# Input projection of an encoder block: a pair's results are made behind the next pair's fourth product, and one of two query or key tiles is convolved in the second half

## The chip, the cores and the metric

The kernel runs on one core of a Trainium2 chip. Five engines with queues of their own work side by side: PE (TensorE, the matrix multiplies), DVE (VectorE), ACT (ScalarE), POOL (GpSimd) and SP (SyncE, which issues all transfers here). The metric is the time of one execution on the device in microseconds (us), lower is better; several executions are run and their median is given.

## The reference, cut to what matters

One layer of a bidirectional encoder block on x of 2048 tokens and 1024 channels. All columns come out of one input projection, and queries and keys go through a short convolution along the tokens:

```python
h = rms_norm(x, norm_pre_g)
proj = einsum('bsd,de->bse', h, w_in)
u_a, z_a, q, k, v, o, z_b, gates, g_a, g_b = split(proj, split_points)
...
qk = silu(centred_depthwise_conv(concatenate([q, k]), conv_qk_w, conv_qk_b))   # 5 taps
q, k = split(qk)
...
h_fwd = mlstm_direction(qh, kh, vh, i_pre[0], f_pre[0])
h_bwd = flip(mlstm_direction(flip(qh), flip(kh), flip(vh), ...))
...
out = einsum('bsd,de->bse', sigmoid(g_a + b_merge[0]) * p_a + sigmoid(g_b + b_merge[1]) * p_b, w_out)
return x + rms_norm(out, norm_post_g)
```

Everything is float32. The change touches only what lies before the recurrences (`mlstm_direction`).

## The kernel before

`phase1` (L434) is the input projection. The tokens are taken in two halves of `HALF` = 1024, each half in two blocks of `BLK` = 512. The columns of the weight are taken in 36 pairs of 128 columns (`in_pairs`, L48). Each pair has a kind: q, k, v and u (a query, key, value or pooling-branch pair) have much to do behind the products, z, o, ga and gb (gates) little; these latter are called light here. The pairs are in a fixed order: ga0 gb0 q0 v0 k0 o0 z0 q1 o1 k1 v1 o2 u0 z1 u1 o3 v2 q2 o4 z2 k2 o5 u2 v3 o6 u3 z3 q3 o7 gb2 k3 ga3 gb3 ga1 gb1 ga2. The first two are computed plainly, the other 34 by a form of Strassen's product (`strassen`, L369): seven products instead of eight, of sums and differences of quarters of the weights (made by DVE at L352, split into a high and a low part by ACT and POOL, L93 and L97) and of x.

A product is 12 matmuls of 128x128 by 128x512 (`mm3`, lines 105 to 107: high by high, high by low, low by high, for four k tiles). The products write to three PSUM banks A, B and C, each with two buffers. Below, P1 to P7 are the seven in the order of the code, of which P2, P4 and P6 use bank B and the engines read the banks like this: ACT copies P1 to `p1`; DVE makes `u2` = bank B + p1 after P2 (L394), and `u3` = bank B + p1 after P4 has been added into the bank (L399). After P6 has been added too, out(2) reads bank B; out(3) reads P3's bank C with u3, out(1) P7's bank C with u2, and out(0) bank A. The out functions make the four tiles of 128 channels by 512 tokens.

`strassen` is a generator, and the main loop interleaves two pairs: `next(this)` issues P1 and P2 of pair i, `run(rest)` issues P6 and P7 of pair i-1 and all that is made of that pair, and the second `next(this)` issues P3, P4, P5 of pair i:

```python
this = work(i, W)
next(this)
run(rest)
next(this)
rest = this
```

So PE sees P1 P2 of a pair, then P6 P7 of the pair before, then P3 P4 P5. P6 of a pair cannot start before u3 of that pair has been read out of bank B.

What is made of a pair: `pair_qk` (L586) has two raw tiles of 128 channels by 1024 tokens (with a halo), and convolves each: ACT makes the first tap with the bias (L602), DVE the other four (L606, scalar_tensor_tensor), ACT a sigmoid (L610), POOL the multiply (L611), SP stores the result. `pair_v` (L613) transposes its raw tiles on PE (L625, 16 transposes of 128x128 into PSUM tiles `vtr`), and ACT and DVE write high and low parts (`vnh`, `vnl`), whose extra columns DVE clears (L618, L619). `pair_u` (L632) makes window sums. The light pairs make a sigmoid and a multiplication or two (L707, L719, L721). Tiles come from pools with three buffers each for raw and acc (all results, among them acc, vnh, vnl, zs, gB) and six for p1, u2, u3.

In the second half the weights are not prepared but reloaded (`again_w`, L308; `keep_w`, L338, stores them in the first). At pairs 10 and later of that half `masked` (L857) makes 32 decay tiles `nm` for a later stage.

The order on each engine is not written by hand: a scheduler places the instructions by the order of the code, by priorities (`tc.high_priority`), by its own timeline of costs and by free buffers; `tc.issue_after(ins)` keeps an instruction behind another. 

Of the kernel before, what the change touches and what calls it, by code (L numbers as in the profile page):

```python
# [77 lines left out]
class Kernel:  # L78
    def __init__(self, ctx, tc, a):
        self.ctx, self.tc, self.nc, self.a = ctx, tc, tc.nc, a  # L80
        self.n = 0
        self.plain = None
        self.free = {}
# [224 lines left out]
    def again_w(self, W, i, wr, wc):  # L308
# [23 lines left out]
        read = nc.sync.dma_start(b22, w_in[i, :, 4:8, P:])  # L332
        put("B22", b22, "pool")
        return read
# [34 lines left out]
    def strassen(self, H, W, psum, pool, out, n=BLK, swap=False):  # L369


        nc = self.nc
# [21 lines left out]
        nc.vector.tensor_tensor(u2, bank["B"], p1, op=ALU.add)  # L394
# [4 lines left out]
        nc.vector.tensor_tensor(u3, bank["B"], p1, op=ALU.add)  # L399
        out(3, bank["C"], u3)  # L400
# [5 lines left out]
        out(2, bank["B"], p1)  # L406
        prod("C", "S4", "B22", False)
        out(1, bank["C"], u2)

# [24 lines left out]
    def phase1(self):  # L434
        tc, nc, a = self.tc, self.nc, self.a
        with ExitStack() as es:
# [6 lines left out]
            wt = es.enter_context(tc.tile_pool(name="wt", bufs=3))  # L443
            po = {t: es.enter_context(tc.tile_pool(name=f"po_{t}", bufs=3)) for t in ("raw", "acc", "p")}
            self.rows = es.enter_context(tc.tile_pool(name="rows", bufs=1))
            self.decay = es.enter_context(tc.tile_pool(name="decay", bufs=2))
# [10 lines left out]
            n = len(self.pairs)  # L457
            for half in range(2):
# [50 lines left out]
                for i in range(2, n):  # L509
# [8 lines left out]
                    with tc.high_priority(offset=200):  # L518
# [3 lines left out]
                        else:  # L522
                            read = self.again_w(W, i, wr, wc)
                    if half == 1:
                        with tc.issue_after(read.ins):
                            for u in range(max(0, 8 * (i - 10) // 6), max(0, min(32, 8 * (i - 9) // 6))):
                                self.masked(u, mask)
# [3 lines left out]
                    this = work(i, W)  # L531
# [3 lines left out]
                    rest = this  # L535
                run(rest)
# [34 lines left out]
    def collect(self, H, W, psum, pool, width, off):  # L571
# [4 lines left out]
        def out(i, ps, add):  # L576
            d = t[i % 2][:, off + (i // 2) * BLK : off + (i // 2 + 1) * BLK]
            if add is None:
                nc.scalar.activation(d, ps, AF.Copy)
            else:  # L580
                nc.vector.tensor_tensor(d, ps, add, op=ALU.add)
# [4 lines left out]
    def pair_qk(self, half, kind, h, H, W, psum, pool):  # L586
        nc = self.nc
        t = yield from self.collect(H, W, psum, pool, HALF + 6, 2 if half == 0 else 4)
        n = HALF - 2 if half == 0 else HALF + 2
        tstart = 0 if half == 0 else HALF - 2  # L590
        dst = self.sp[f"{kind}T{h}"]
        for i in range(2):
            raw = t[i]
            ct = (8 if kind == "k" else 0) + 2 * h + i
            if half == 0:
                nc.vector.memset(raw[:, 0:2], 0.0)  # L596
                nc.vector.tensor_copy(self.halo_qk[:, ct, :], raw[:, HALF - 2 : HALF + 2])
            else:
                nc.vector.tensor_copy(raw[:, 0:4], self.halo_qk[:, ct, :])
                nc.vector.memset(raw[:, HALF + 4 : HALF + 6], 0.0)  # L600
            acc = pool.tile([P, HALF + 2], F32, tag="acc", name=self.nm("acc"))
            nc.scalar.activation(  # L602
                acc[:, :n], raw[:, 0:n], AF.Identity, scale=self.cw[:, ct, 0:1], bias=self.cb[:, ct : ct + 1]
            )
            for tap in range(1, TAPS):
# [4 lines left out]
            nc.scalar.activation(raw[:, :n], acc[:, :n], AF.Sigmoid)  # L610
            nc.gpsimd.tensor_tensor(acc[:, :n], acc[:, :n], raw[:, :n], op=ALU.mult)  # L611
            nc.sync.dma_start(dst[:, i, tstart : tstart + n], acc[:, :n])
# [55 lines left out]
    def pointwise(self, H, W, psum, pool, body):  # L668
# [3 lines left out]
        def out(i, ps, add):  # L672
            if add is None:
                body(i % 2, i // 2, ps)
            else:
                nc.vector.tensor_tensor(add, ps, add, op=ALU.add)
                body(i % 2, i // 2, add)

        yield from self.strassen(H, W, psum, pool, out)

    def pair_z(self, half, kind, g, H, W, psum, pool):
        nc = self.nc
        o = [pool.tile([P, HALF], F32, tag="acc", name=self.nm("zs")) for _ in range(2)]

        def body(i, b, x):
            d = o[i][:, b * BLK : (b + 1) * BLK]
# [7 lines left out]
    def pair_g(self, half, kind, g, H, W, psum, pool):  # L694
# [4 lines left out]
        def out(i, ps, add):  # L699
# [3 lines left out]
            else:  # L703
                x = d = add
                nc.vector.tensor_tensor(x, ps, add, op=ALU.add)
# [3 lines left out]
            nc.sync.dma_start(dst[:, i % 2, t0 : t0 + BLK], d)  # L709

        yield from self.strassen(H, W, psum, pool, out)

    def pair_o(self, half, kind, j, H, W, psum, pool):
        nc = self.nc
        o = [pool.tile([P, HALF], F32, tag="acc", name=self.nm("gB")) for _ in range(2)]

        def body(i, b, x):
            d = o[i][:, b * BLK : (b + 1) * BLK]
# [8 lines left out]
    def spills(self):  # L727
# [11 lines left out]
        for i in range(2, len(self.pairs)):  # L739
            sp[f"wt{i}"] = self.dram(f"wt{i}", [P, 4, 2, 4 * P])  # L740
        for j in range(8):
# [793 lines left out]
```

## Time and profile before

| | us |
|---|---|
| median of 3 executions | 2410.05 (2406.89 to 2412.60) |
| the profiled execution, its own time | 2414.79 |
| its span in the trace | 2413.0 |
| PE busy | 2325.3 (96%) |
| DVE busy | 1477.7 (61%) |
| POOL busy | 1139.3 (47%) |
| ACT busy | 895.5 (37%) |

Busy time is the time in which an engine executes an instruction; the span is from the first to the last record of the trace. In a timeline, a row gives the start, the duration, the instruction with its output and inputs, and in square brackets how long the engine was idle before it and which instruction's end released it. A matmul's duration overlaps that of the next, so the step from start to start is the measure there. The input projection fills about the first 1430 us, half of it each of the two halves of the tokens.

### The profile page before, as it was taken

To read this page: it belongs to the slowest core of one execution; us is meant where nothing else is said; L and a number is where in the kernel's file an instruction comes from. 1 tells how busy PE (TensorE), PEld (TensorE's weight loads), DVE (VectorE), ACT (ScalarE), POOL (GpSimd) and SP (SyncE) were. 2 spreads that over 40 slices of the span, in tenths; PEclk is the share of its full clock that TensorE was granted. 3 is DMA by queue.
4 is the path that set the end of the run, shared out by engine and by line. 5 is a ranking of instruction groups with operands and counts; after the bars stand their busy time and mean duration, and the time that the engine had idled before them with its cause. 6 is when DMAs were issued, how large, how long until landed. Compare 5 with 4: busy or idle time off the path is not lost. (4 is left out here: it accounts for less than half of the span.)

```text
span 2413.0 us, 35767 instructions
## 1 busy us (share of the span) xinstructions
PE 2325.3 (96%) x12569; PEld 2003.2 (83%) x12569; DVE 1477.7 (61%) x2495; ACT 895.5 (37%) x1773; POOL 1139.3 (47%) x902
## 2 busy tenths in 40 slices
PE   7998999999999999999999999998999999999998
PEld 5777788887878778888888887997989899999776
DVE  6886766887875465534465433887985333354765
ACT  5434333433334333222322333776764112121442
POOL 4655655564655423544454430554564211233775
PEclk9999999999999999999999999999999999999999
DMA  4457565556684466787777766766656546588763
GB/s 155 167 207 240 205 237 214 219 173 220 219 278 171 141 191 201 235 264 233 246 227 241 253 226 232 228 209 216 205 184 212 173 154 200 182 282 278 250 218 122
DMA packets 300707, 513.24 MB, mean 213 GB/s; under 512 B 27248, under 2 KB 137968, under 8 KB 300528
## 3 DMA queue, kind: packets, MB, share of 16 engines
q1 hardware_dynamic: 300528, 510.97, 63.4%
q8 instruction: 99, 1.62, 0.3%
q14 instruction: 80, 0.66, 0.1%
HBM read 314.25 MB, written 196.61 MB: 212 GB/s over the span
## 5 line engine op out<-in xcount | busy, mean ns | idle before, releaser
L606 DVE SCALAR_TENSOR_TENSOR acc<-raw,conv_w,acc 128x1022 f32<-128x1022 f32 (+1 forms) x128 | 219.0, 1735 | 10.4 <-ACT acc L602 6.9
L97 POOL TENSOR_TENSOR wB21l<-wraw,wB21h 128x512 fp32r<-128x512 f32 x76 | 109.8, 1445 | 228.4 <-ACT wB21h L93 200.5
L1159 POOL TENSOR_TENSOR qs<-q,isc 128x256 f32<-128x256 f32 x120 | 92.2, 771 | 143.3 <-PE num L1175 62.6
L97 POOL TENSOR_TENSOR wB22l<-wraw,wB22h 128x512 fp32r<-128x512 f32 x76 | 118.0, 1552 | 81.6 <-ACT wB22h L93 61.9
L885 PE MATMUL pb<-oxs,w_proj_mlstml 128*128 128x256 f32 x512 | 143.8, 281 | 0.0
L884 PE MATMUL pb<-oxs,w_proj_mlstmh 128*128 128x256 f32 x512 | 143.8, 281 | 0.0
L884 PE MATMUL paps<-pys,w_proj_poolh 128*128 128x256 f32 x512 | 143.4, 282 | 0.2 <-POOL pys L97 0.2
L883 PE MATMUL pb<-oxs,w_proj_mlstmh 128*128 128x256 f32 x512 | 143.5, 280 | 0.0
L883 PE MATMUL paps<-pys,w_proj_poolh 128*128 128x256 f32 x512 | 142.3, 282 | 0.6 <-DVE sga L1012 0.6
L885 PE MATMUL paps<-pys,w_proj_pooll 128*128 128x256 f32 x512 | 142.1, 282 | 0.0
L394 DVE TENSOR_TENSOR u<-bankB,p 128x512 f32<-128x512 f32 x76 | 52.1, 686 | 138.6 <-PE bankB L107 128.9
L97 POOL TENSOR_TENSOR wB11l<-wraw,wB11h 128x512 fp32r<-128x512 f32 x72 | 109.8, 1526 | 40.5 <-ACT wB11h L93 39.1
L105 PE MATMUL bankB<-A22h,wT4h 128*128 128x512 f32 x272 | 108.5, 399 | 14.0 <-DVE u L399 14.0
L611 POOL TENSOR_TENSOR acc<-acc,raw 128x1022 f32<-128x1022 f32 (+1 forms) x32 | 79.6, 2487 | 71.1 <-ACT raw L610 63.7
L105 PE MATMUL bankC<-S1h,wT1h 128*128 128x512 f32 x272 | 107.6, 395 | 3.4 <-ACT sg L707 3.4
L105 PE MATMUL bankB<-S3h,wT3h 128*128 128x512 f32 x272 | 106.2, 390 | 2.7 <-DVE u L394 2.7
L107 PE MATMUL bankB<-A22h,wT4l 128*128 128x512 f32 x272 | 108.0, 397 | 0.0
L106 PE MATMUL bankB<-A22l,wT4h 128*128 128x512 f32 x272 | 108.0, 397 | 0.0
L107 PE MATMUL bankB<-S2h,wT2l 128*128 128x512 f32 x272 | 106.7, 392 | 1.2 <-DVE raw L596 1.2
L107 PE MATMUL bankC<-S1h,wT1l 128*128 128x512 f32 x272 | 107.2, 394 | 0.0
L105 PE MATMUL bankB<-S2h,wT2h 128*128 128x512 f32 x272 | 107.1, 394 | 0.0
L106 PE MATMUL bankC<-S1l,wT1h 128*128 128x512 f32 x272 | 106.9, 393 | 0.0
(438 smaller groups left out, 7662.5 us busy)
## 6 DMA issues: line engine op xcount, KB each, us to landing
wraw<-in_w_in SPq DMA_DIRECT2D x110, 512.0 KB, 4.3
wt<-wT2h SPq DMA_DIRECT2D x34, 256.0 KB, 3.5
wt<-wT1h SPq DMA_DIRECT2D x34, 256.0 KB, 3.7
wt<-wT3h SPq DMA_DIRECT2D x34, 256.0 KB, 3.8
wt<-wT2l SPq DMA_DIRECT2D x34, 256.0 KB, 3.6
wt<-wT1l SPq DMA_DIRECT2D x34, 256.0 KB, 3.6
wt<-wT3l SPq DMA_DIRECT2D x34, 256.0 KB, 2.6
wt<-wT4h SPq DMA_DIRECT2D x34, 256.0 KB, 2.0
```

The lines of the kernel that those rows point to most:

```text
L97: return eng.tensor_tensor(lo, x, hi.bitcast(F32), op=ALU.subtract)
L105: nc.tensor.matmul(ps, wh, xh, start=start and kt == 0, stop=False, skip_group_check=True)
L106: nc.tensor.matmul(ps, wh, xl, start=False, stop=False, skip_group_check=True)
L107: nc.tensor.matmul(ps, wl, xh, start=False, stop=stop and kt == 3, skip_group_check=True)
L394: nc.vector.tensor_tensor(u2, bank["B"], p1, op=ALU.add)
L606: nc.vector.scalar_tensor_tensor(acc[:, :n], raw[:, tap : tap + n], self.cw[:, ct, tap : tap + 1], acc[:, :n], op0=ALU.mult, op1=ALU.add,)
L611: nc.gpsimd.tensor_tensor(acc[:, :n], acc[:, :n], raw[:, :n], op=ALU.mult)
L883: nc.tensor.matmul(ps, wh, xh, start=i == 0, stop=False)
L884: nc.tensor.matmul(ps, wh, xl, start=False, stop=False)
L885: nc.tensor.matmul(ps, wl, xh, start=False, stop=i == n)
L1159: nc.gpsimd.tensor_tensor(qs[d], q[:, :, ck], isc[:, d, j % 2, None, :].to_broadcast([P, 2, P]), op=ALU.mult)
```

## The change

Two things are changed. First, `strassen` yields once more behind u3 and once at its end, and the loop has more steps: P1, P2 of pair i; P6, P7 of pair i-1; P3, P4 and u3 of pair i; then what is made of pair i-1; then out(3), P5 and out(0) of pair i. Second, in the first half only tile 0 of each q or k pair is convolved; the raw tile 1 is stored to DRAM. In the second half it is loaded again into a pool with one buffer of its own, `late` (`late_load`, behind pair i's last weight load, from pair 5 on), and convolved (`conv`) in a later light pair, each tap kept behind one of the four DVE instructions of that pair that read banks (`read_banks`). So 8 tiles are convolved at another time, with 8 stores and 8 loads of 512 KB more. Besides, zs and gB tiles are taken when first written, nm lives in the pool of the weight differences (three buffers) instead of decay's two, and decay has one buffer.

```diff
@@ strassen
-        nc.vector.tensor_tensor(u2, bank["B"], p1, op=ALU.add)
+        self.read_banks.append(nc.vector.tensor_tensor(u2, bank["B"], p1, op=ALU.add))
         yield
         prod("C", "S1", "T1", True)
         prod("B", "S3", "T3", False)
         u3 = pool.tile([P, n], F32, tag="p", name=self.nm("u3"))
-        nc.vector.tensor_tensor(u3, bank["B"], p1, op=ALU.add)
-        out(3, bank["C"], u3)
+        self.read_banks.append(nc.vector.tensor_tensor(u3, bank["B"], p1, op=ALU.add))
+        yield
+        self.read_banks.append(out(3, bank["C"], u3))
         if not self.edge:
             prod("A", "A12", "B21", False)
             out(0, bank["A"], None)
         yield
         prod("B", "A22", "T4", False)
-        out(2, bank["B"], p1)
+        self.read_banks.append(out(2, bank["B"], p1))
         prod("C", "S4", "B22", False)
         out(1, bank["C"], u2)
+        yield
...
@@ phase1
+            late, waits = [(kind, h) for h in range(NH) for kind in "qk"], None
...
-                    this = work(i, W)
+                    this, self.read_banks = work(i, W), []
+                    next(this)
+                    next(rest, None)
                     next(this)
                     run(rest)
                     next(this)
                     rest = this
+                    if half == 1 and waits is not None and i >= 7 and self.pairs[i][0] not in "qkuv":
+                        kind, h, raw = waits
+                        self.conv(pool, kind, h, 1, raw, HALF - 2, 0, self.read_banks)
+                        waits = None
+                    elif half == 1 and waits is None and late and i >= 5:
+                        with tc.issue_after(self.read.ins):
+                            waits = self.late_load(*late.pop(0))
...
@@ pair_qk
             if half == 0:
-                nc.vector.memset(raw[:, 0:2], 0.0)
                 nc.vector.tensor_copy(self.halo_qk[:, ct, :], raw[:, HALF - 2 : HALF + 2])
+                if i == 1:
+                    nc.sync.dma_start(self.sp[f"raw{kind}{h}"], raw[:, 2 : HALF + 2])
+                else:
+                    nc.vector.memset(raw[:, 0:2], 0.0)
+                    self.conv(pool, kind, h, i, raw, HALF - 2, 0)
...
+    def conv(self, pool, kind, h, i, raw, n, tstart, ties=()):
...
+        for tap in range(1, TAPS):
+            with self.tc.issue_after(ties[tap - 1].ins) if ties else ExitStack():
                 nc.vector.scalar_tensor_tensor(
                     acc[:, :n], raw[:, tap : tap + n], self.cw[:, ct, tap : tap + 1], acc[:, :n],
                     op0=ALU.mult, op1=ALU.add,
                 )
...
+    def late_load(self, kind, h):
+        raw = self.late.tile([P, HALF + 2], F32, tag="late", name=self.nm("late"))
+        self.nc.vector.memset(raw[:, 0:2], 0.0)
+        self.nc.sync.dma_start(raw[:, 2:], self.sp[f"raw{kind}{h}"])
+        return kind, h, raw
...
@@ masked
-        t = self.decay.tile([P, 2, 2, P], F32, tag="nm", name=self.nm("nm"))
+        t = self.wt_pool.tile([P, 2, 2, P], F32, tag="wt", name=self.nm("nm"))
```

What this does to the order of the engines is shown at three places. The first is DVE's queue in the first half where q1 (raw_1674 and raw_1675, with the accumulators acc_1918 and acc_1929) meets u3 of o1 (u_311_1962). Before, from q1's last raw on:

```order
L581 TENSOR_TENSOR raw_1675<-bankC_1678,u_270_1705 128x512
L606 SCALAR_TENSOR_TENSOR acc_1918<-raw_1674,conv_w,acc_1918 128x1022 x2
L606 SCALAR_TENSOR_TENSOR acc_1929<-raw_1675,conv_w,acc_1929 128x1022
L606 SCALAR_TENSOR_TENSOR acc_1918<-raw_1674,conv_w,acc_1918 128x1022
L352 TENSOR_TENSOR wt_2152<-wraw_2134,wraw_2132 128x512
L606 SCALAR_TENSOR_TENSOR acc_1929<-raw_1675,conv_w,acc_1929 128x1022
L399 TENSOR_TENSOR u_311_1962<-bankB_1860,p_307_1874 128x512
L606 SCALAR_TENSOR_TENSOR acc_1918<-raw_1674,conv_w,acc_1918 128x1022
L606 SCALAR_TENSOR_TENSOR acc_1929<-raw_1675,conv_w,acc_1929 128x1022
L676 TENSOR_TENSOR u_311_1962<-bankC_1861,u_311_1962 128x512
L606 SCALAR_TENSOR_TENSOR acc_1929<-raw_1675,conv_w,acc_1929 128x1022
```

And now, with the lines of the changed kernel (L595 is out of a q, k or v pair, L628 a tap, L400 u3, L705 and L756 belong to o1); tile 0's accumulator is acc_1935:

```order
L595 TENSOR_TENSOR raw_1668<-bankC_1671,u_268_1698 128x512
L628 SCALAR_TENSOR_TENSOR acc_1935<-raw_1667,conv_w,acc_1935 128x1022 x3
L352 TENSOR_TENSOR wt_2136<-wraw_2118,wraw_2116 128x512
L628 SCALAR_TENSOR_TENSOR acc_1935<-raw_1667,conv_w,acc_1935 128x1022
L400 TENSOR_TENSOR u_305_1931<-bankB_1851,p_303_1865 128x512
L705 TENSOR_TENSOR u_305_1931<-bankC_1852,u_305_1931 128x512
L756 TENSOR_TENSOR gB_1948<-u_305_1931,gB_1948 128x512
L98 TENSOR_TENSOR wT2l_2129<-wt_2126,wT2h_2128 128x512
L395 TENSOR_TENSOR u_335_2043<-bankB_2015,p_334_2029 128x512
```

Two accumulators were worked on side by side, five taps ahead of u3 and three behind it; now there is one, with all four taps ahead of u3.

The second place is PE's queue in the first half, where v0 (raw_992 and raw_993) is transposed while k0 is computed. Before, at the start of P3 of k0 (bankC_1165):

```order
L105 MATMUL bankC_1165<-S1h_393,wT1h_1129 128x512
L106 MATMUL bankC_1165<-S1l_394,wT1h_1129 128x512
L625 MATMUL vtr_1224<-ident,raw_992 128x128
L625 MATMUL vtr_1231<-ident,raw_992 128x128
L107 MATMUL bankC_1165<-S1h_393,wT1l_1130 128x512
L105 MATMUL bankC_1165<-S1h_393,wT1h_1129 128x512
```

and at the end of its P4 (bankB_1164):

```order
L105 MATMUL bankB_1164<-S3h_395,wT3h_1135 128x512
L106 MATMUL bankB_1164<-S3l_396,wT3h_1135 128x512
L625 MATMUL vtr_1224<-ident,raw_993 128x128
L625 MATMUL vtr_1224<-ident,raw_992 128x128
L625 MATMUL vtr_1224<-ident,raw_993 128x128
L625 MATMUL vtr_1231<-ident,raw_993 128x128
L625 MATMUL vtr_1231<-ident,raw_992 128x128
L625 MATMUL vtr_1231<-ident,raw_993 128x128
L107 MATMUL bankB_1164<-S3h_395,wT3l_1136 128x512
L105 MATMUL bankA_1163<-A12h_389,wB21h_1139 128x512
```

Now (raw_1003 and raw_1004, L654) at the end of P4:

```order
L108 MATMUL bankB_1166<-S3h_406,wT3l_1138 128x512
L654 MATMUL vtr_1252<-ident,raw_1003 128x128
L654 MATMUL vtr_1252<-ident,raw_1004 128x128
L654 MATMUL vtr_1252<-ident,raw_1003 128x128
L654 MATMUL vtr_1252<-ident,raw_1004 128x128
L654 MATMUL vtr_1259<-ident,raw_1003 128x128
L654 MATMUL vtr_1259<-ident,raw_1004 128x128
L654 MATMUL vtr_1259<-ident,raw_1003 128x128
L654 MATMUL vtr_1259<-ident,raw_1004 128x128
L106 MATMUL bankA_1165<-A12h_400,wB21h_1141 128x512
```

The first two transposes moved from the start of P3 to the end of P4, and the other six from ahead of P4's last matmul to behind it.

The third place is DVE's queue in the second half, in the changed kernel only, where the late convolution of light pair o1 (late_7389, acc_7908) meets the next pair, k1; L395 is u2 and L400 u3 of k1, and the L705 and L756 belong to o1:

```order
L395 TENSOR_TENSOR u_1391_7980<-bankB_7952,p_1390_7966 128x512
L705 TENSOR_TENSOR p_1361_7800<-bankB_7786,p_1361_7800 128x512
L705 TENSOR_TENSOR u_1362_7814<-bankC_7787,u_1362_7814 128x512
L628 SCALAR_TENSOR_TENSOR acc_7908<-late_7389,conv_w,acc_7908 128x1022
L756 TENSOR_TENSOR gB_7892<-u_1362_7814,gB_7892 128x512
L628 SCALAR_TENSOR_TENSOR acc_7908<-late_7389,conv_w,acc_7908 128x1022 x2
L400 TENSOR_TENSOR u_1392_8035<-bankB_7952,p_1390_7966 128x512
L628 SCALAR_TENSOR_TENSOR acc_7908<-late_7389,conv_w,acc_7908 128x1022
L595 TENSOR_TENSOR raw_7950<-bankC_7953,u_1392_8035 128x512
```

Three of the four late taps, which are new here, stand between u2 and u3 of k1, and the fourth behind u3.

## Rows read from the trace of the kernel before

**Rows 1.** The page: busy time and share of each engine.

```profile
PE 2325.3 (96%) x12569; PEld 2003.2 (83%) x12569; DVE 1477.7 (61%) x2495; ACT 895.5 (37%) x1773; POOL 1139.3 (47%) x902
```

**Rows 2.** Windows: PE, PEld, DVE, ACT, POOL busy, clock, DMA share, GB/s.

```profile
200.00:300.00 100.00, 87.99 (x367) 70.65 (x366) 76.15 (x84) 42.20 (x69) 58.98 (x36) 0.95 0.63 222
900.00:1000.00 100.00, 100.00 (x445) 82.85 (x444) 56.83 (x62) 33.43 (x50) 44.45 (x26) 1.00 0.68 218
```

**Rows 3.** Waits of PE, 60 to 760 us: total, times, longest.

```profile
PE bankB L105 <- DVE u L399: 13.2, 4, 4.7
...
PE vtr L625 <- DVE vnh L618: 3.2, 2, 1.6
...
PE vtr L625 <- DVE raw L581: 1.3, 1, 1.3
PE vtr L625 <- ACT raw L579: 1.2, 2, 0.8
```

**Rows 4.** Waits of PE, 760 to 1440 us.

```profile
PE vtr L625 <- DVE vnl L97: 2.6, 2, 2.5
PE vtr L625 <- DVE raw L581: 1.5, 1, 1.5
```

**Rows 5.** Timeline of PE: start, us, instruction, [idle before <-releaser].

```profile
212.96 0.79 PE L105 MATMUL bankB<-A22h,wT4h 128*128 128x512 f32 x1 [4.70 <-DVE u L399]
...
221.30 0.39 PE L105 MATMUL bankC<-S1h,wT1h 128*128 128x512 f32 x1
...
237.26 0.50 PE L105 MATMUL bankB<-A22h,wT4h 128*128 128x512 f32 x1 [2.20 <-DVE u L399]
...
239.21 0.39 PE L107 MATMUL bankB<-A22h,wT4l 128*128 128x512 f32 x1
...
278.90 0.50 PE L105 MATMUL bankB<-A22h,wT4h 128*128 128x512 f32 x1 [2.99 <-DVE u L399]
...
281.24 0.63 PE L107 MATMUL bankB<-A22h,wT4l 128*128 128x512 f32 x1
...
286.12 0.39 PE L105 MATMUL bankC<-S1h,wT1h 128*128 128x512 f32 x1
...
716.92 0.50 PE L105 MATMUL bankB<-A22h,wT4h 128*128 128x512 f32 x1 [3.31 <-DVE u L399]
```

**Rows 6.** Timeline of DVE, q1's taps.

```profile
225.74 7.97 DVE L606 SCALAR_TENSOR_TENSOR acc<-raw,conv_w,acc 128x1022 f32<-128x1022 f32 x4
```

**Rows 7.** Source line L606, 900 to 1400 us: ns min/median/max.

```profile
L606 DVE SCALAR_TENSOR_TENSOR acc<-raw,conv_w,acc x49: 1273/1289/3436, 899.9 to 1399.0; 128x1026 f32<-128x1026 f32 x49
```

**Rows 8.** Timeline of DVE, k1's taps.

```profile
269.63 5.74 DVE L606 SCALAR_TENSOR_TENSOR acc<-raw,conv_w,acc 128x1022 f32<-128x1022 f32 x3
```

**Rows 9.** Timeline of PE, transposes of v0 and v1.

```profile
140.88 0.88 PE L625 MATMUL vtr<-ident,raw 128*128 128x128 f32 x6 [1.54 <-DVE vnh L618]
...
294.08 0.88 PE L625 MATMUL vtr<-ident,raw 128*128 128x128 f32 x6 [1.64 <-DVE vnh L618]
```

**Rows 10.** Timeline of DVE, v0 of the first half.

```profile
133.60 0.07 DVE L619 MEMSET vnl<- 128x8 f32 x1 [0.52 <-DMA qT<-acc]
...
135.56 0.06 DVE L596 MEMSET raw<- 128x2 f32 x1 [1.26 <-POOL acc L611]
```

**Rows 11.** DVE groups, 800 to 1420 us: busy, mean ns, idle before.

```profile
L394 DVE TENSOR_TENSOR u<-bankB,p 128x512 f32<-128x512 f32 x31 | 21.3, 688 | 97.3 <-PE bankB L107 90.9 <-issue 6.4
L399 DVE TENSOR_TENSOR u<-bankB,p 128x512 f32<-128x512 f32 x30 | 20.6, 686 | 33.1 <-PE bankB L107 33.1
```

**Rows 12.** Timeline of POOL near 209 us.

```profile
209.27 1.27 POOL L97 TENSOR_TENSOR wT4l<-wt,wT4h 128x512 fp32r<-128x512 f32 x1 [3.58 <-ACT wT4h L93]
```

**Rows 13.** Timeline of DVE, a light pair of the second half.

```profile
967.84 3.44 DVE L606 SCALAR_TENSOR_TENSOR acc<-raw,conv_w,acc 128x1026 f32<-128x1026 f32 x1
...
980.56 0.69 DVE L399 TENSOR_TENSOR u<-bankB,p 128x512 f32<-128x512 f32 x1 [3.06 <-PE bankB L107]
...
988.79 0.69 DVE L394 TENSOR_TENSOR u<-bankB,p 128x512 f32<-128x512 f32 x1 [6.74 <-PE bankB L107]
```

More of the change, by code (lines that the diff above doesn't have):

```diff
@@ L82, in __init__ @@
         self.plain = None
+        self.read_banks = []
         self.free = {}
@@ L522, in phase1 @@
                         else:
-                            read = self.again_w(W, i, wr, wc)
+                            self.again_w(W, i, wr, wc)
                     if half == 1:
-                        with tc.issue_after(read.ins):
+                        with tc.issue_after(self.read.ins):
                             for u in range(max(0, 8 * (i - 10) // 6), max(0, min(32, 8 * (i - 9) // 6))):
@@ L600, in pair_qk @@
                 nc.vector.memset(raw[:, HALF + 4 : HALF + 6], 0.0)
[L601 to L605, printed above, removed]
+                self.conv(pool, kind, h, i, raw, HALF + 2, HALF - 2)
+    def conv(self, pool, kind, h, i, raw, n, tstart, ties=()):
+        nc = self.nc
+        ct = (8 if kind == "k" else 0) + 2 * h + i
+        acc = pool.tile([P, HALF + 2], F32, tag="acc", name=self.nm("acc"))
+        nc.scalar.activation(
+            acc[:, :n], raw[:, 0:n], AF.Identity, scale=self.cw[:, ct, 0:1], bias=self.cb[:, ct : ct + 1]
+        )
+        for tap in range(1, TAPS):
+            with self.tc.issue_after(ties[tap - 1].ins) if ties else ExitStack():
                 nc.vector.scalar_tensor_tensor(
@@ L682, in pair_z @@
         nc = self.nc
-        o = [pool.tile([P, HALF], F32, tag="acc", name=self.nm("zs")) for _ in range(2)]
+        o = []
         def body(i, b, x):
+            if not o:
+                o.extend(pool.tile([P, HALF], F32, tag="acc", name=self.nm("zs")) for _ in range(2))
             d = o[i][:, b * BLK : (b + 1) * BLK]
@@ L709, in out @@
             nc.sync.dma_start(dst[:, i % 2, t0 : t0 + BLK], d)
+            return None if add is None else read
         yield from self.strassen(H, W, psum, pool, out)
@@ L714, in pair_o @@
         nc = self.nc
-        o = [pool.tile([P, HALF], F32, tag="acc", name=self.nm("gB")) for _ in range(2)]
+        o = []
         def body(i, b, x):
+            if not o:
+                o.extend(pool.tile([P, HALF], F32, tag="acc", name=self.nm("gB")) for _ in range(2))
             d = o[i][:, b * BLK : (b + 1) * BLK]
@@ L740, in spills @@
             sp[f"wt{i}"] = self.dram(f"wt{i}", [P, 4, 2, 4 * P])
+        for h in range(NH):
+            for kind in "qk":
+                sp[f"raw{kind}{h}"] = self.dram(f"raw{kind}{h}", [P, HALF])
         for j in range(8):
```

28 lines of the change are left out of this document (13 added, 15 removed).

## The prediction

> **What bounds the kernel now.** I read the page first. PE is busy for 96% of the span [rows 1], so the time can move only where PE stands idle, where it runs at the lower clock, or where it gets another amount of work. The change gives PE the same instructions as before. Beyond the input projection (which fills the first 1430 us) no engine's order differs, so everything is decided there. The windows come next [rows 2]: in the second half PE is busy 100.00 of 100 us with 445 matmuls, so one matmul step is 100/445 = 0.225 us. In the first half, between 200 and 300 us, PE is busy only 87.99 us, its granted clock averages 0.95, and DVE is at 76.15 us. That window also holds the start of the q/k pairs.
>
> Then the waits of PE alone. In the first half [rows 3] the largest group is bankB waiting for the DVE instruction u3 of L399, 13.2 us in four waits. P6 of the pair before cannot write into bank B before u3 has read it, and u3 stands in DVE's queue behind convolution taps. The transposes of v (vtr) wait 3.2 us for vnh, 1.2 for ACT's raw and 1.3 for DVE's raw. In the second half there are just two groups, 2.6 and 1.5 us [rows 4]. These rows make 23 us in all, and only those waits that the change touches count.
>
> The four u3 waits one by one [rows 5]: 4.70 us before 212.96, 2.20 before 237.26, 2.99 before 278.90, 3.31 before 716.92. A long wait costs twice. After the 2.99 us the granted clock falls to the lower level: a matmul that takes 0.39 us at full clock takes 0.63 at 281.24, and the 24 matmuls of P6 and P7 from 278.90 to 286.12 take 7.22 us instead of 24 x 0.225 = 5.40, so 1.8 more. After the 2.20 us wait the matmuls stay at 0.39 (239.21). After the 4.70 us wait the 24 take 8.34, so 2.9 more.
>
> **The change part by part.**
>
> *One tile of two convolved in the first half.* The waits at 237.26 and 278.90 belong to o1 behind q1 and to v1 behind k1. The order shows for the first that five taps stand between q1's last raw and u3 of o1 before, and four afterwards, none of them behind u3. The weight difference (L352) stays between them. Four taps there took 7.97 us, so 1.99 each [rows 6]; a tap alone takes 1.29, the median of the second half [rows 7]. One tap fewer is worth 1.29 to 1.99; beside the same POOL work I take 1.7. **Term 1, q1/o1: -1.7** of 2.20, without clock. **Term 2, k1/v1:** three taps took 5.74, so 1.91 each [rows 8]; again -1.7 of 2.99. That leaves 1.3 us, less than the 2.20 after which no clock was lost, so the 1.8 us of clock come back too: -3.5. Bounds: -1.3 to -2.0 for term 1, and for term 2 -1.3 (a tap, and the clock falls all the same) to -4.8 (the whole wait).
>
> *What is made of a pair stands later.* This concerns v, whose 16 transposes are PE work. Before, in v0 of the first half, the first two of eight transposes stand behind the second matmul of P3 and wait 0.77 us for a raw of ACT (part of the 1.2 us group [rows 3]); afterwards all eight stand behind the last matmul of P4, 22 matmuls or 5 us later for these two, so that wait goes. The other six move by one matmul only, 0.2 us; what they wait 1.54 us for [rows 9] is DVE's last raw. Before, clears that wait for a store and for POOL's multiply stand ahead of it in DVE's queue [rows 10]; afterwards they don't, but two weight differences more do. I take half, 0.8. **Term 3, v0: -1.6** (0 to -2.3). **Term 4, v1:** 0.5 and 1.64 [rows 3, 9]; DVE's queue still holds clears of v's buffers, which wait for a store, ahead of raw. Half again, -0.9 (0 to -2.1). **Term 5, v3:** the 1.3 us on DVE's raw [rows 3]; DVE is behind with u2's window sums, which the change leaves, -0.2 (0 to -1.3). **Term 6, v0 of the second half:** 2.6 and 1.5 [rows 4]. u3 and the reading of bank C now stand ahead of the two vnl, 2 x 0.69 us later (20.6 us over 30 of them [rows 11]), against 3 more matmuls that PE has by then, 0.68. I take +0.7 (-2.5 to +2.5).
>
> *What stays.* The 4.70 us at 212.96: DVE waits there for a weight difference whose buffer POOL frees late, and POOL's instruction waited 3.58 us for ACT [rows 12]; none of these moves, 0. The 3.31 at 716.92 lies behind x of the second half (five L193), in the same order after: 0.
>
> *The second half gets eight convolutions.* 32 taps of 1.29 us are 41 us of DVE, put into a stretch in which DVE is busy 56.83 of 100 us [rows 2] and idles 97.3 us ahead of u2 and 33.1 ahead of u3 while PE works [rows 11]. That idle time is the cover. The dangerous place is the pair behind a light one, where three late taps stand ahead of u3, as the third order listing shows. Take k1 around 980 us, the pair of that listing [rows 13]: u3 starts at 980.56 as soon as P4 ends; PE needs the bank only after P5, P1 and P2, whose end shows as the start of the next u2, 988.79. Were all three taps to begin only at 980.56, u3 would end at 980.56 + 3 x 1.29 + 0.69 = 985.1, which leaves 3.7 us. Nothing is lost: 0. If the cover went, three taps would cost what lies above these 3.7 us.
>
> *DMAs.* Eight stores and eight loads of 512 KB, 8.4 MB against 513 MB, on SP's queue while the DMA engines are 0.63 to 0.68 busy [rows 2]; each load has a pair or more (some 19 us) before its taps: 0. The lazily taken zs and gB tiles and nm's buffers: 0 by the same cover; they gate nothing that PE waits for in these rows.
>
> **Sum:** -1.7 - 3.5 - 1.6 - 0.9 - 0.2 + 0.7 = -7.2 us. Against the profiled execution's own 2414.8 that gives 2407.6; this one lay 4.7 above the median 2410.05, so by the median's level the forecast is **2403 us**. With every bound taken favourably it is -2.0 - 4.8 - 2.3 - 2.1 - 1.3 - 2.5 = -15.0, unfavourably -1.3 - 1.3 + 2.5 = -0.1.
>
> **A rule against it.** In the trace one tap of the second half took 3.44 us against 1.29 [rows 13, 7], so something can hold a tap 2.15 us. The Trainium skill, page "SBUF — State Buffer", section "SBUF: two separate sides", says that VectorE with two SBUF inputs and a GpSimd instruction that reads SBUF lock each other out of a shared port pair for a whole instruction. The trace agrees in kind with this 3.44. By the rule every late tap could be held by a POOL instruction, and the change would cost time instead of nothing; by the medians it costs nothing.
>
> **Rivals.**
>
> *R1, no change that can be measured.* The waits merely pass over: u3 of o1 and v1 still has four taps at 1.9 and the weight difference ahead, the transposes wait for vnh wherever they stand. For it: DVE at 76% in that window [rows 2], and POOL-stretched taps. Against it: one tap less is certain in the order. The sum is then between -1.3 x 2 and -4.5: 2406 to 2411.
>
> *R2, slower.* The late taps are held beside POOL. Three of 3.44 are 10.3 us against 3.9, 6.5 more, above the 3.7 of slack by 2.8; with lost clock (1.8) 4.6 us a convolution. From 3.7 us of extra hold (two of three taps) it decides. In half of the eight it costs 18 us, 2421; in all, 37 us, 2440. Against it: the median of 49 taps is 1.289 [rows 7] and POOL is busy 44.45% there [rows 2].
>
> *R3, more gain.* With half of the convolution gone from the first half, ACT and POOL come earlier, and the 4.70 + 2.9 at 212.96 or the 3.31 at 716.92 with slow matmuls behind it (1.8, as behind 278.90) shrink: 5 to 10 us beyond the forecast, 2393 to 2398. Against it: the chains there [rows 12] aren't made of convolution work in the order.
>
> **How the numbers follow.** Forecast 0.51 (own range 2398 to 2406), R1 0.26, R2 0.11, R3 0.12. A measurement tells about 0.2%, 4.8 us. Faster: R3 and nearly all of the forecast, 0.61 with a little of R1's edge; same 0.28; slower 0.11. The range from 2395 to 2411 leaves out R2 and about half of R3.
>
> **What would show it.** Waits of PE on u3 near 237 and 279 fall below 1 and 1.5 us, and no 0.63 us matmuls follow the second; the vtr waits of v0 in the first half fall to about a third; the wait at 212.96 stays near 4.7; in the second half the taps read from late show a median near 1.3 us, and PE has no wait for u3. I am wrong if u3 waits appear behind the light pairs of the second half, if the four taps in the first half take longer apiece than the five did, or if the total goes with a place that I put at zero.

## The result, and the profile after

The changed kernel takes 2399.68 us (median of 7, 2394.49 to 2403.61) against 2410.05 (2406.89 to 2412.92): the ratio is 0.9947, interval 0.9936 to 0.9959. It is 10.4 us faster; 2403 was forecast, with a gain of 7. The execution in the trace took 2403.61 us, with a span of 2401.8, which is 11.2 below that of before. In both traces the input projection lasts longer than the 1430 us given above: its last matmul ends at 1490.5 us before and at 1478.7 after.

The first lines of its page, and the windows that answer to [rows 1, 2]; the columns are those of before. The last fence is a third window of before, for comparison:

```profile
span 2401.8 us, 35786 instructions
...
PE 2321.7 (97%) x12569; PEld 2004.0 (83%) x12569; DVE 1480.2 (62%) x2495; ACT 895.1 (37%) x1773; POOL 1147.0 (48%) x902
```

```profile
200.00:300.00 100.00, 97.48 (x438) 80.48 (x438) 66.27 (x80) 42.69 (x73) 54.98 (x36) 1.00 0.69 245
900.00:1000.00 100.00, 98.31 (x437) 80.99 (x436) 55.20 (x62) 30.84 (x44) 52.07 (x30) 1.00 0.72 227
1200.00:1300.00 100.00, 96.63 (x428) 79.58 (x426) 59.91 (x71) 25.13 (x39) 60.43 (x38) 0.98 0.76 252
```

```profile
1200.00:1300.00 100.00, 100.00 (x451) 82.79 (x450) 49.31 (x64) 25.18 (x39) 49.21 (x36) 1.00 0.75 239
```

Where [rows 2] had 87.99 us of PE between 200 and 300 us, there are 97.48, and the clock is back at 1.00. But the second half, full before, now has holes. The waits of PE say the same; first those of 60 to 760 us [rows 3], then those of 760 to 1440 [rows 4]:

```profile
PE bankC L106 <- ACT sg L739: 3.4, 1, 3.4
PE bankB L106 <- DVE u L400: 2.5, 1, 2.5
PE bankB L106 <- DVE u L395: 1.3, 1, 1.3
PE bankB L108 <- DVE wT2l L98: 1.1, 1, 1.1
```

```profile
PE bankB L106 <- DVE u L400: 6.1, 2, 3.4
PE vtr L654 <- DVE vnl L98: 5.2, 1, 5.2
PE vtr L654 <- DVE raw L595: 2.7, 2, 1.7
```

Of 13.2 us that PE waited for u3 in the first half, 2.5 are left, and v's transposes wait no more there. In the second half 6.1 us for u3 are new, and v's waits grew from 4.1 to 7.9.

A ledger shows it place by place: the time from the first matmul of one pair's P1 to that of the next, taken from PE's timeline of both kernels, for the pairs that differ. A pair without a wait takes 19.04 us, one with v's transposes in it 19.98. "o1" is the stretch of o1, in which P6 and P7 of the pair before it (q1) run.

```
first half    k0     o1     k1     o2     o6     gb2    ga1    start to second half
before        22.78  26.80  21.81  27.48  23.38  19.42  24.27  687.74
after         19.94  19.04  21.85  19.99  19.96  19.04  19.04  660.57

second half   k0     o0     o2     q2     k2     v3     to the last pair
before        21.78  25.06  19.94  20.02  19.04  19.04  697.09
after         21.52  28.03  21.88  23.02  19.45  24.32  710.69
```

So the first half gave 27.2 us and the second took back 13.6. Together with 1.8 us more at the start (79.9 before the first such pair, 81.74 now; 80.0 to 82.1 in other traces of these kernels) this makes the 11.7 us by which the last pair begins earlier; later stages lose 0.5.

What took the time in the second half, at its dearest place, v3, on DVE, ACT and PE in turn (start, duration, instruction, idle before it):

```profile
1209.38 0.69 DVE L705 TENSOR_TENSOR u<-bankC,u 128x512 f32<-128x512 f32 x1 [2.03 <-PE bankC L108]
1218.18 1.28 DVE L628 SCALAR_TENSOR_TENSOR acc<-late,conv_w,acc 128x1022 f32<-128x1022 f32 x1 [8.11 <-ACT acc L623]
1219.38 1.79 DVE L756 TENSOR_TENSOR gB<-u,gB 128x512 f32<-128x512 f32 x1
1221.10 4.56 DVE L628 SCALAR_TENSOR_TENSOR acc<-late,conv_w,acc 128x1022 f32<-128x1022 f32 x2
1225.58 0.68 DVE L400 TENSOR_TENSOR u<-bankB,p 128x512 f32<-128x512 f32 x1
```

```profile
1216.90 1.25 ACT L623 ACTIVATE acc<-late,conv_b,conv_w 128x1022 f32<-128x1022 f32 x1 [4.89 <-DMA kT<-acc]
```

```profile
1214.62 0.39 PE L106 MATMUL bankA<-A12h,wB21h 128*128 128x512 f32 x1
...
1226.31 0.50 PE L106 MATMUL bankB<-A22h,wT4h 128*128 128x512 f32 x1 [3.37 <-DVE u L400]
...
1228.48 0.63 PE L107 MATMUL bankB<-A22l,wT4h 128*128 128x512 f32 x1
```

The late tile has been loaded, but its accumulator is one of three result buffers, and ACT's first tap (L623) waits until a store of k's result has emptied it. DVE is idle 8.11 us. Then three taps stand ahead of u3 and end 3.4 us too late; the granted clock falls behind that (0.51 between 1227.7 and 1231 us, the level of 1.2 GHz, with 0.63 us for a matmul), and the pair takes 24.32 us.

The late start is not all of it. The second of the two merged taps took 3.26 us where a tap alone takes 1.29, beside a multiplication on POOL that belongs to the light pair:

```profile
1222.40 3.26 DVE L628 SCALAR_TENSOR_TENSOR acc<-late,conv_w,acc 128x1022 f32<-128x1022 f32 x1
```

```profile
1221.30 3.27 POOL L759 TENSOR_TENSOR gB<-gB,gB 128x1024 f32<-128x1024 f32 x1 [0.68 <-POOL wB21l L98]
```

### The profile page after: what moved, and what is told of

It reads as the page before. It is cut to its first block, busy times and chain, and to the rows that moved or that the text cites. A ratio compares the mean times of both kernels' runs of the same rounds, so it can differ in the third digit from the quotient of the medians.

```text
span 2401.8 us, 35786 instructions
## 1 busy us (share of the span) xinstructions
PE 2321.7 (97%) x12569; PEld 2004.0 (83%) x12569; DVE 1480.2 (62%) x2495; ACT 895.1 (37%) x1773; POOL 1147.0 (48%) x902
## 4 chain that ended last, share of the span: by engine, by line
PE 67%; DMA 11%; DVE 10%; POOL 4%; issue 4%; ACT 3%; SPq 1%; POOLq 0%; DVEq 0%; ACTq 0%
PE bankB L106 6%; PE bankB L107 6%; PE bankB L108 6%; PE bankC L107 4%; PE bankC L106 4%; PE bankC L108 4%; PE bankA L108 4%; PE bankA L107 4%; PE bankA L106 4%; PE num L1213 4%; DVE acc L628 3%; PE pb L922 2%; PE pb L921 2%; PE pb L923 2%; DMA negM<-nm 2%
## 5 line engine op out<-in xcount | busy, mean ns | idle before, releaser
L628 DVE SCALAR_TENSOR_TENSOR acc<-raw,conv_w,acc 128x1026 f32<-128x1026 f32 (+1 forms) x96 | 153.3, 1610 | 11.3 <-ACT acc L623 8.9
L905 POOL TENSOR_TENSOR nm<-nm,mask 128x256 f32<-128x256 f32 x64 | 63.5, 1007 | 93.1 <-DMA nm<-negM 86.4
L395 DVE TENSOR_TENSOR u<-bankB,p 128x512 f32<-128x512 f32 x76 | 52.1, 686 | 90.4 <-PE bankB L108 78.0
L107 PE MATMUL bankB<-S2l,wT2h 128*128 128x512 f32 x272 | 107.3, 395 | 0.0
L106 PE MATMUL bankA<-A12h,wB21h 128*128 128x512 f32 x272 | 106.7, 392 | 0.0
```

Source lines behind the costliest of these rows:

```text
L106: nc.tensor.matmul(ps, wh, xh, start=start and kt == 0, stop=False, skip_group_check=True)
L107: nc.tensor.matmul(ps, wh, xl, start=False, stop=False, skip_group_check=True)
L395: self.read_banks.append(nc.vector.tensor_tensor(u2, bank["B"], p1, op=ALU.add))
L628: nc.vector.scalar_tensor_tensor(acc[:, :n], raw[:, tap : tap + n], self.cw[:, ct, tap : tap + 1], acc[:, :n], op0=ALU.mult, op1=ALU.add,)
L905: nc.gpsimd.tensor_tensor(t[:, d, :, :], t[:, d, :, :], mask[:, d, None, :].to_broadcast([P, 2, P]), op=ALU.add)
```

## The experiments

Kernels run once are compared by the ledger, since single executions of one kernel differ by up to 9 us. The ledger has its own spread: of two kernels that were traced twice (both below), one took 658.3 and 662.6 us in the first half and 701.2 and 702.5 in the second, the other 659.8 and 659.0, and 701.3 and 699.9. Nearly all of the 4.3 us is at one place, k1 (19.59 and 23.99). The kernel before, run beside them, took 2413.0 us with the first three experiments, 2415.3 with the four on the late convolutions' cost and v0 that ran once, 2414.2 with the fourth buffer and the two kernels of five and six executions, and 2408.6 with the last two.

**Which part gives the first half's gain.** Both tiles convolved in the first half again:

```diff
-                if i == 1:
-                    nc.sync.dma_start(self.sp[f"raw{kind}{h}"], raw[:, 2 : HALF + 2])
-                else:
-                    nc.vector.memset(raw[:, 0:2], 0.0)
-                    self.conv(pool, kind, h, i, raw, HALF - 2, 0)
+                nc.vector.memset(raw[:, 0:2], 0.0)
+                self.conv(pool, kind, h, i, raw, HALF - 2, 0)
...
-            late, waits = [(kind, h) for h in range(NH) for kind in "qk"], None
+            late, waits = [], None
```

> The changed kernel with both query and key tiles convolved in the first half again (no late convolutions, loads or stores); the new order of the loop, the lazy tiles and the pools stay. In the changed kernel the first half ended 25.3 us earlier than before and the second half lost 13.6. Theory 1 (the convolution that is gone gives the first half's gain; the order gives only v's transposes): the first half gains about 4 us, the waits for u3 near 213, 237 and 279 us come back with 4 to 5, 2 and 3 us, the second half loses only 3 us at v0, total about 2409 us. Theory 2 (the order gives it): the first half keeps about 20 of 25 us, total about 2392 us.

2412.3 us (2413.0 for the kernel before beside it). The first half took 689.5 us, and the waits are those of before (PE, 60 to 760 us):

```profile
PE bankB L106 <- DVE u L400: 12.1, 4, 5.1
PE vtr L651 <- DVE vnh L644: 6.1, 2, 3.6
```

Theory 1 holds, and more sharply than expected: the new order alone (with the result tiles taken late and the other pools) gives nothing that shows, and v's waits (3.2 and 1.2 us before) are longer in this trace.

The other way round, the loop of before with the late convolutions:

```diff
                     next(this)
-                    next(rest, None)
-                    next(this)
                     run(rest)
                     next(this)
+                    next(this)
```

> The changed kernel with the loop of before (P6, P7 and what is made of the pair in one step ahead of P3); late convolutions, lazy tiles and pools stay. Theory 1 (the missing convolution gives the gain): the first half keeps 17 to 21 of 25 us, v0's transposes wait 2.3 us again; the second half loses 11 us to late taps but not the 3 us at v0; total about 2402 us. Theory 2 (the order gives it): the first half gains 5 us at most, total about 2415 us.

2397.1 us; first half 659.8, second 709.9, against 660.6 and 710.7. Theory 1 again, but v's transposes don't wait in the first half, and o0 in the second takes 28.3 us also here: neither v's gain nor the 3 us at o0 comes from the order. It moves single waits; the sum stays.

**The result tiles taken when first written**, which I had put at nothing, taken early again:

```diff
-        o = []
+        o = [pool.tile([P, HALF], F32, tag="acc", name=self.nm("eo")) for _ in range(2)]
```

> The changed kernel with the z and o pairs' result tiles taken at the pair's start, as before. Theory A (a result tile taken early holds the buffer that the loads of x need, so that ACT waits for x ahead of a weight part and DVE behind it: the 4.70 us before 212.96 with 2.9 us of slow matmuls): the wait near 210 us comes back, 7 to 8 us longer in the first half, about 2407 us. Theory B (the convolution that is gone frees those buffers): the wait stays gone, within 1 us of the changed kernel there, about 2400 us.

2398.8 us; o1 takes 19.05 us, so theory A falls.

**What the late convolutions cost.** This kernel leaves the convolution of tile 1 out for the first half's tokens; the raw tile goes to the result's place.

```diff
-                    nc.sync.dma_start(self.sp[f"raw{kind}{h}"], raw[:, 2 : HALF + 2])
+                    nc.sync.dma_start(self.sp[f"{kind}T{h}"][:, 1, 0 : HALF - 2], raw[:, 2:HALF])
...
-            late, waits = [(kind, h) for h in range(NH) for kind in "qk"], None
+            late, waits = [], None
```

> The changed kernel without the eight late convolutions and their loads in the second half; tile 1 of each query and key pair goes, not convolved, straight to the result's place for the first half's tokens, so that this work is left out. Theory C (the late convolutions cost the second half about 10 us: u3 or v's last raw behind late taps): the waits at v1, v2, u2 (1.9, 3.0, 5.3 us) are gone, the 3 us at v0 stay, total about 2389 us. Theory D (the new order of the loop makes them): they stay, about 2400 us.

2388.3 us. The second half takes 700.5 us instead of 710.7: 10.2 us, and o2, q2, k2 and v3 are at 19.94, 19.94, 19.04 and 19.04. Theory C. o0 stays at 28.9.

**Why they cost that.** One word is changed, the pool of the late accumulator:

```diff
-        acc = pool.tile([P, HALF + 2], F32, tag="acc", name=self.nm("acc"))
+        acc = pool.tile([P, HALF + 2], F32, tag="raw" if ties else "acc", name=self.nm("acc"))
```

> The changed kernel, but a late convolution's accumulator comes from the raw tiles' pool (idle in light pairs) instead of the results' pool. Theory E (the taps come late because their accumulator waits for the store of an earlier result, and so three of them stand in front of the next pair's u3): now each tap stands behind its own bank reader in the light pair, the waits at v2 and u2's successors fall from 3.0 + 5.3 to below 1 us together, total about 2392 us. Theory F (DVE hasn't the time, or POOL holds the taps, wherever they stand): the second half still loses about 10 us, total about 2400 us.

2386.4 us, second half 701.2, only 0.7 more than with no late convolution at all (2.1 more in a second trace). q2, k2 and v3 are at 19.98, 19.04 and 19.04; o2 stays 1.5 us longer, at 21.44. Theory E for three of the four places. The view of the tile `late` counts how long an engine sat idle ahead of work on that tile, and whose end it waited for. The line of ACT's first tap (L623) is the one to read, in the changed kernel and then here (us, times):

```profile
  DVE acc L628: 46.4, 8
  ACT acc L623: 35.2, 8
```

```profile
  DVE acc L628: 19.5, 7
...
  ACT acc L623: 0.9, 2
```

The taps now stand behind the bank reader that each was tied to, and the next u3 waits only for PE:

```profile
1191.76 2.31 DVE L628 SCALAR_TENSOR_TENSOR acc<-late,conv_w,acc 128x1022 f32<-128x1022 f32 x1
1194.00 0.68 DVE L705 TENSOR_TENSOR u<-bankC,u 128x512 f32<-128x512 f32 x1
...
1198.07 2.31 DVE L628 SCALAR_TENSOR_TENSOR acc<-late,conv_w,acc 128x1022 f32<-128x1022 f32 x1
...
1207.89 0.69 DVE L400 TENSOR_TENSOR u<-bankB,p 128x512 f32<-128x512 f32 x1 [0.44 <-PE bankB L108]
```

The same with the loop of before:

> The same with the loop of before (P6, P7 and what is made of the pair in one step). If the order of the loop is worth nothing once the late taps stand well: within 2 us of the kernel with the new loop, both near 2391 us. If the new order is what gives the late taps room: the waits for u3 in the second half are larger here, total about 2396 us.

2391.7 us in a single execution, with 659.8 and 701.3 in the two halves (658.3 and 701.2 with the new loop). Both were then timed again, with five and six executions:

> The changed kernel with the late accumulators from the raw pool, timed against the kernel before. By its one look (2386.4) and the ledger of the pairs (first half 29 us shorter, second half 4 us longer than before): 2386 us, ratio 0.990. If the one look was lucky: 2392 us, ratio 0.9925.

> The same with the loop of before. If the order of the loop is worth nothing: within 2 us of the kernel with the new loop. If it is worth what the two first looks differ by: 5 us slower. By the ledger of the pairs, where the input projection ends 1440.7 us in the one and 1442.9 us in the other, I expect 2 us.

2391.02 us, ratio 0.9901 (0.9886 to 0.9915), and 2388.26, ratio 0.9904 (0.9889 to 0.9919). The order of the loop is worth nothing that this measures, with the late convolutions as (by one trace, above) without.

**v0 of the second half.**

```diff
-            nc.vector.memset(hi[:, :, DH:].bitcast(F32), 1.0)
-            nc.vector.memset(lo[:, :, DH:].bitcast(F32), 0.0)
+            nc.gpsimd.memset(hi[:, :, DH:].bitcast(F32), 1.0)
+            nc.gpsimd.memset(lo[:, :, DH:].bitcast(F32), 0.0)
```

> The changed kernel with the clears of v's extra columns (vnh, vnl) on POOL instead of DVE. Theory G (at v0 of the second half DVE stands 9.4 us behind such a clear, which waits for a store of q, and u3, the bank reads and the low parts behind it are late, which costs the transposes 5.2 us): that wait falls by 3 us or more, total about 2396 us. Theory H (the transposes wait for the tile that the clear opens, whoever clears it): the 5.2 us stay, total about 2400 us.

2401.7 us; o0 takes 29.0. Theory G falls: it doesn't matter which engine clears. H is not shown by it either. Behind the clear stood a scan of row math that waits for a small transfer, and in this trace that scan holds DVE just as long, 10.08 us instead of 9.40:

```profile
860.39 1.35 DVE L861 TENSOR_TENSOR_SCAN rows<-rows 4x16 f32<-4x16 f32 x2 [10.08 <-DMA rows<-ends]
```

So two waits of about the same length lie one behind the other there, and taking one away shows nothing. Both taken away was not tried.

**Why a convolution fewer helps the first half.** A fourth result buffer for the kernel with both tiles in the first half:

```diff
-                        shape, dt, tag=tag, name=name, bufs=bufs or (6 if tag == "p" else 3)
+                        shape, dt, tag=tag, name=name, bufs=bufs or {"p": 6, "acc": 4}.get(tag, 3)
```

> Both tiles convolved in the first half, no late convolution (as in the run without late convolutions), but four instead of three buffers for results, among which are the accumulators, v's high and low parts and the tiles of x that are read for the second half's statistics. Theory I (a convolution fewer helps because it holds a result buffer less: x's tiles and v's parts wait for stores): the 5.1 us at o1 with its slow matmuls and v's waits of 2.5 and 3.6 us go, the first half falls from 689 to about 673 us, total about 2397 us. Theory J (it helps by the time of DVE, POOL and ACT): the waits stay, first half about 689 us, total about 2411 us.

2417.8 us; first half 685.8. Each theory is right for a part. o1 falls from 26.79 to 19.28 us, so its wait was one for buffers. SP's first loads of x there, before, in the changed kernel and with the fourth buffer, show how (q1 begins at 183.6, 182.6 and 185.2 us):

```profile
190.80 0.38 SPq L164 DMA_DIRECT2D xs<-in_x  x1
197.36 0.33 SPq L164 DMA_DIRECT2D xs<-in_x  x1
```

```profile
183.64 0.38 SPq L165 DMA_DIRECT2D xs<-in_x  x1
189.19 0.33 SPq L165 DMA_DIRECT2D xs<-in_x  x1
```

```profile
192.31 0.87 SPq L165 DMA_DIRECT2D xs<-in_x  x2
```

With a convolution fewer the first load goes 7 us earlier; with a fourth buffer two go at once. But k1 rises from 23.70 to 28.05, since u3 of o1 is then what comes late, and v's waits and ga1 stay. A fourth result buffer does not help those.

The waits at o1 and k1 have a common neighbour: the tiles of x for the second half's statistics are loaded from pair 8 (o1) on, into result buffers, and ACT waits for them ahead of weight parts. So their place was moved, in the best kernel so far, and alone in the kernel before:

```diff
-                    if half == 0 and i == 8:
+                    if half == 0 and i == 18:
```

> The changed kernel with the late accumulators from the raw pool, and the statistics of the second half's x begun at pair 18 (o4, a light one) instead of pair 8 (o1). Theory K (the wait for u3 of o1 that stays in the changed kernel, 0.3 to 3 us in six traces, comes from q1's last raw, which stands on DVE behind weight differences whose parts ACT makes behind a wait for x's tiles): the wait at k1 goes, 1 to 5 us less in the first half, 2384 to 2388 us, ratio 0.987 to 0.989. Theory L (four taps beside POOL and the weight difference make it): the wait stays near 2 us, and x's tiles may make another one at pairs 18 to 20; 2389 us or more, ratio 0.990 or above.

2381.35 us, ratio 0.9879 (0.9862 to 0.9895), the lowest ratio here, though its interval overlaps that of the same kernel with the statistics at pair 8 (0.9886 to 0.9915). k1 takes 19.04 us, where the nine other traces with one tile in the first half have 19.59 to 23.99. Theory K; all of PE's waits between 60 and 760 us are now at q0, the start:

```profile
PE bankC L106 <- ACT sg L739: 3.4, 1, 3.4
PE bankB L106 <- DVE u L395: 1.8, 1, 1.8
PE bankA L106 <- ACT p L389: 1.7, 1, 1.7
PE bankB L108 <- DVE wT2l L98: 1.1, 1, 1.1
```

> The kernel before with nothing changed but the statistics of the second half's x at pair 18 instead of pair 8. Theory K: the 4.7 us at o1 with their slow matmuls (7.8 us a pair) go and the 2.2 us at k1 with them or stay, first half 678 to 681 us instead of 687.7, total 2403 us, ratio 0.9965 - if no new wait appears at pairs 18 to 20. Theory M (convolutions of q0 and k0 hold back whatever uses their buffers, whenever it comes): a wait like that appears at q2 and k2's neighbours, total 2410 us.

2399.74 us, ratio 0.9957 (0.9942 to 0.9972). The first half takes 678.0 us. The waits at o1 and k1 (7.8 and 2.8 us over 19.04) are gone, o2's falls from 27.48 to 25.59, and new ones at z2 to o5 cost 4.5. Both theories hold in part. This one number gives nearly what the whole change gave.

## Why the prediction came out, and which of its steps did not

The total was right and the direction too; the balance behind it was not. Forecast were -7.9 us for the first half and +0.7 for the second; the ledger shows -27.2 and +13.6. Two errors in opposite directions cancelled, so the total was luck. Of the prediction's own signs three came: no wait and no slow matmul where the 2.99 us were, no waits of v0's transposes in the first half, and a median of 1.28 us for a late tap. Three did not: the wait near 237 us stayed, the one at 212.96 went, and u3 is waited for behind light pairs of the second half.

- **Terms 2 and 4, k1/v1 (o2's stretch): -3.5 and -0.9 forecast, -7.5 measured.** Both were sized too small; nothing of the waits is left. For term 2 the mechanism was right: with a tap fewer, from the start of k1's last raw to the end of u3 DVE takes 9.4 us instead of 11.6, the stall ends and the clock comes back. For term 4 it was not: I gave it to the later place of v's transposes, but with the new order and both tiles in the first half they still wait 3.6 us there (o2 26.83), and with the old order and one tile they don't (20.03).
- **Term 3, v0: -1.6 forecast, -2.8 measured.** The gain is there but not the reason, which was again the later place of v's transposes. With the new order and both tiles in the first half k0 still takes 22.68 us; with the old order and one tile, 20.00. It comes from the convolution that is gone; whether by DVE's or POOL's time was not tried.
- **Term 1, u3 of o1: -1.7 forecast, nothing measured (21.81 to 21.85).** The saved tap is there: from the start of q1's last raw to the end of u3 DVE takes 12.07 us before and 9.83 after. But that raw starts 3.84 us behind the end of P7 before (221.30, the start of P3) and 6.39 behind it after (212.53): PE no longer stands still at o1, which had hidden how late DVE was (with the fourth buffer, too, o1's wait goes and k1's grows). I took the taps ahead of u3 as all that makes it late; what came late was the start of the taps. In the changed kernel q1's last raw stands behind weight differences, one of which waits 2.12 us for a part from POOL, which waits for ACT, which waits for x's tiles. With the statistics elsewhere and the same four taps ahead of u3 the wait is 0, and so it is in the kernel before with five. The size of this wait differs between traces of one kernel (k1, above). DVE before, then the start of P3 after, then DVE after:

```profile
225.14 0.68 DVE L581 TENSOR_TENSOR raw<-bankC,u 128x512 f32<-128x512 f32 x1
...
236.53 0.68 DVE L399 TENSOR_TENSOR u<-bankB,p 128x512 f32<-128x512 f32 x1
```

```profile
212.53 0.39 PE L106 MATMUL bankC<-S1h,wT1h 128*128 128x512 f32 x1
```

```profile
214.01 0.69 DVE L352 TENSOR_TENSOR wt<-wraw,wt 128x512 f32<-128x512 f32 x1 [2.12 <-POOL wT1l L98]
...
218.92 0.69 DVE L595 TENSOR_TENSOR raw<-bankC,u 128x512 f32<-128x512 f32 x1
219.52 5.74 DVE L628 SCALAR_TENSOR_TENSOR acc<-raw,conv_w,acc 128x1022 f32<-128x1022 f32 x3
...
228.07 0.68 DVE L400 TENSOR_TENSOR u<-bankB,p 128x512 f32<-128x512 f32 x1
```

- **"None of these moves, 0", o1: -7.8 measured; ga1: -5.2.** This was the dearest failed step. Rival R3 named both places, though it gave them to ACT's and POOL's own work. I read that the chain behind the 4.70 us had no convolution in its instructions, and took that as no link. The link is a buffer: convolutions and x's tiles share three result buffers, and a fourth buffer takes the wait away as a convolution fewer does. For ga1 a fourth result buffer doesn't help (25.32 us); that it is k3's convolution, which precedes it on DVE, follows only from the waits' going with it.
- **Term 5, v3 in the first half: -0.2 forecast, -3.4 measured at o6.** It goes with the convolution too (23.69 without late convolutions, 20.01 with them and the old loop). Which instruction freed DVE there wasn't tried.
- **"Nothing is lost: 0" for the late taps: +10.2 measured.** The idle time of DVE is there, as [rows 11] said. The failed step is the bound "Were all three taps to begin only at 980.56", which is where P4 ends. At v3 P4 ended at 1214.6 and the first tap began at 1218.18, 3.6 us later, since I asked only when DVE is free and not when the accumulator is. That uses up the forecast's 3.7 us of slack, but no more: three taps of 1.29 and u3 would have ended at 1222.7, and PE stood still from 1222.9 on. The 3.37 us came on top of it, from instructions stretched beside POOL (the tap of 3.26 us) and from the light pair's gB (1.79 us) among the taps. Rival R2 had the place (three taps ahead of u3), a price near (4.6 us a convolution forecast, 5.3 at v3, 3.0 at q2) and at v3 a part of the mechanism; it lacked the late start. With the accumulator elsewhere taps that are stretched as much cost no wait for u3.
- **Taps beside POOL** were stretched, but that alone did not decide. By the timelines of DVE and POOL in the second half of the changed kernel, 59 taps with POOL at work for over 30% of their time took 1.80 us on average, 37 others 1.29. With the accumulator elsewhere it is the same (60 taps 1.75, 36 taps 1.29), and the waits of u3 are gone. The rule on the shared port of the Trainium skill (page "SBUF — State Buffer", section "SBUF: two separate sides") fits the stretch; the averages do not prove it.
- **Term 6, v0 of the second half: +0.7 forecast, +2.7 measured** (k0 and o0 together). Not the place of u3: the old loop has it too. All ten traces with one tile in the first half have 27 us or more at o0 (27.0 to 29.0), the others 22.5 to 25.9. The store of q0's result, for which the clear waits by the trace, takes 9.3 us to land before and 11.2 after (9.7 to 12.5 in those ten traces, 8.0 to 9.4 in the others). Why it takes longer stays open, and so does how much of the wait is the store's and how much the row math's.

## What to carry to other kernels

A wait has two questions, when the engine is free and when its buffer is; idle time on an engine is room for moved work only if the moved work's tiles come from a pool that is idle there too. When a stall's chain has none of the changed work in its instructions, look at the pools before writing zero: work that is removed frees buffers, and a load far away starts earlier. And undo each half of a change alone: here one half did everything, the other nothing that could be measured, and a single number beside them, where the statistics begin, gave nearly as much as both.

## What the runs showed of the hardware that was not expected

A 512 KB store of q took 11.2 us to land at 850.66 us in the changed kernel, where such stores take 3.9 us in the median between 900 and 1400 us of the kernel before. In the stretch from 848 to 861 us the 16 DMA engines were often busy and moved little, 316 of 693 packets being under 512 bytes, while a 1 KB transfer of the row math was under way (busy tenths, then GB/s, in 40 slices of the 13 us):

```profile
DMA  0419876996601849212600532498002313257776
GB/s 0 3 13 69 221 176 221 176 57 6 6 0 6 44 13 25 19 32 57 69 13 19 50 57 57 82 158 101 32 13 6 13 6 19 38 151 284 303 290 279
DMA packets 693, 1.03 MB, mean 80 GB/s; under 512 B 316, under 2 KB 316, under 8 KB 692
```

That the small packets hold the store is likely, and was not tested.

The length of a wait alone does not tell whether the clock falls behind it. Behind waits for u3 of 2.99 us (before, 278.90) and 3.37 (after, 1226.31) matmuls fell to 0.63 us for a stretch, behind 2.20 (before, 237.26) they did not. But they fell behind 2.75 us too (both tiles in the first half, 239.50; granted clock 0.72 from 240 to 246 us), and not behind 3.08 (the kernel before with the statistics at pair 18, 710.58; 1.00 from 711 to 720) or 3.12 (the old loop with the late convolutions, 1225.3; 1.00 from 1225.5 to 1235). So the prediction's step "less than the 2.20 after which no clock was lost, so the 1.8 us of clock come back too" was not a safe one, though it came out.
